# Two attentions over sixteen meta tokens: their products widened to all 128 rows of the array

## The chip, the core and the metric

The kernel runs on one core of one Trainium2 chip. The metric is device time in microseconds, from one launch. A core has a matrix engine (TensorE, "PE" in the profile, with its weight loads as "PEld"), a vector engine (VectorE, "DVE"), a scalar engine (ScalarE, "ACT"), GpSimd ("POOL") and a queue engine that issues transfers (SyncE, "SP"). They run side by side and wait for each other by semaphores. TensorE's clock has two levels, 1.2 and 2.4 GHz; the profile shows which was granted as 0.50 or 1.00.

## What is computed

Two layers over 272 tokens: 16 learned meta tokens, then 256 tokens of input. Each layer has a SwiGLU block, a token mixer and a second SwiGLU block, each with norms and a residual. The mixer runs two attentions on one projection of its input and adds them under two gates. Cut to what matters here:

```python
def fox_attention(q, k, v, log_f, key_valid):      # 8 heads of 64
    s = einsum('bhqd,bhkd->bhqk', q, k) * scale + cum_q - cum_k
    p = softmax(where(allowed, s, -inf))            # causal, blocks of 128
    return einsum('bhqk,bhkd->bhqd', p, v)

def gla_chunked(q, k, v, log_a):                    # 4 heads, keys 64, values 128, chunks of 128
    cb = cumsum(log_a)                              # per key feature
    inter = einsum('bhtk,bhkv->bhtv', q * exp(cb), state)
    att = einsum('bhtk,bhsk,bhtsk->bhts', q, k, exp(cb_t - cb_s))
    return inter + einsum('bhts,bhsv->bhtv', att, v)
```

A query of the first chunk of 128 input tokens sees the 16 meta tokens and the earlier tokens of its chunk; one of the second chunk sees the meta tokens, the whole first chunk and the earlier tokens of its own. The last layer's output of the meta tokens isn't needed.

## The kernel before

Everything is float32. The large products (projections, SwiGLU) split each weight tile into two parts (ScalarE casts at line 106, VectorE subtracts at line 112) and run three products of 128 rows by 128 columns each over 272 tokens (lines 122 to 124; 256 tokens where the meta tokens' output isn't needed). The attentions' own products take plain float32 operands; each of them stands in the trace as two passes, so that one product is two records.

The mixer (`mixer`) walks over the 33 blocks of the input projection. Before each block it issues what earlier blocks made possible: the table at lines 768 to 788 says before which block each step stands. A list scheduler then orders every engine's instructions; it may move small steps among the projection's products. SyncE loads weights ahead; GpSimd clears tiles and takes powers for the norms.

The steps that the change touches, for one layer:

- `turn_gla` (line 456): transposes the values of one of the four heads of the gated linear attention and copies them to `gv[0]` (16 meta tokens), `gv[1]`, `gv[2]` (the chunks), at line 462.
- `between_decays` (line 591) makes the decayed queries and keys between tiles (`ex`, 2 x 416 columns): the meta keys once decayed to the end of the meta tokens (for the first chunk) and once to the end of the first chunk (for the second).
- `between` (line 605) multiplies them: per head two products of 64 rows by 16 columns over 128 queries (line 612, meta keys with either chunk) and one of 64 rows by 128 columns (line 614, first chunk's keys with the second chunk's queries). Heads 0 and 2 lie in the lower 64 rows, heads 1 and 3 in the upper. Two copies bring the first kind to `am` (16 partitions, 512 columns each).
- `gla_values` (line 718): for chunk 1 and chunk 2, per head, a product with `am` (16 rows by 128 columns over 128 values), for chunk 2 one with `abc`, and one with `att` (128 by 128), all summed in PSUM (line 727).
- `weigh` (line 664), once per pair of heads of the forgetting attention: a product of the meta keys' weights `ptm` with `fvm` (32 rows by 128 columns over 256, line 667), then products with 64 columns for each head (lines 671 and 672).
- `products` and `diagonal` (lines 520 and 565), which the change leaves alone: the decayed products inside the chunks, level by level, 64 rows high (lines 535, 550, 553, 576, 578).

Around the mixer stands the norm: `Post.done` calls `inv_rms` (line 164), in which GpSimd takes a power at line 180 that the next products wait for. GpSimd clears `vm` for the mixer (line 433) just ahead of the power that ends the first SwiGLU block.

Of the kernel before, what the change touches and what calls it, by code (L numbers as in the profile page):

```python
# [27 lines left out]
# Columns of a weight tile as loaded, and as split; how many tiles of both kinds.  # L28
# [20 lines left out]
def hybrid_kernel(ctx: ExitStack, tc: tile.TileContext, xT, w_in, w_al, w_fg, w_o, w_gu1, w_dn1, w_gu2, w_dn2, w_end, g_end, vecs, consts, marks, out):  # L49
# [43 lines left out]
    # The operands of a first product, in the order of their use.  # L93
# [32 lines left out]
    def mm2(o, w, col, x, start, stop):  # L126
        """For a block whose columns 64.. repeat those before: they take the lower parts of the weights."""
        a = w[0][:, col : col + P]
        nc.scalar.copy(a[:, 64:], w[1][:, col + 64 : col + P].bitcast(F32))
        nc.tensor.matmul(o, a, x[0], start=start, stop=False)  # L130
        nc.tensor.matmul(o, a, x[1], start=False, stop=stop)

    def run(items, nk, narrow=None):
        """Products of consecutive blocks of a weight tile: (output, operand, number in its sum), nk in a sum."""
# [10 lines left out]
    def block(src, o, xh, xl, c0):  # L145
        """128 output features."""
# [3 lines left out]
    def group(srcs, outs, xh, xl, c0, narrow=None):  # L150
        """Four times 128 output features, the contraction outermost: a tile holds two rows of blocks, feature-minor."""
# [5 lines left out]
    def idle(after, k):  # L157
        """Products that nothing uses, so that the array's clock isn't throttled while it waits."""
# [5 lines left out]
    def inv_rms(parts, n, factor, warm=False):  # L164
        """factor / rms of a token, on every partition: a PSUM tile [P, n]."""
# [23 lines left out]
    def prep(l, gcol, c0, yg=None, rb=None):  # L189
        """h += yg * rb; x = h * gain in two float32r parts; 1/rms of h, per token."""  # L190
# [28 lines left out]
    class Post:  # L219
        """Takes the output blocks of a sublayer; then gives what the residual needs."""  # L220
# [28 lines left out]
    def finish(fp, hh, hl):  # L249
        """The last products and norm, tokens on the partitions."""  # L250
# [84 lines left out]

    def operands():
        """Tiles for queries and keys: rows 64.. pick a head's cumulated gate, of the query or of the key."""
# [8 lines left out]
    def mixer(l, xh, xl, rs, qa, ka, c0):  # L346
# [6 lines left out]
        with tc.tile_pool(name="mix", bufs=1) as mp, tc.tile_pool(name="tmp", bufs=2) as tp:  # L353
            wal = mp.tile([16, GH * GDK], F32, name="wal")
            nc.sync.dma_start(wal, w_al[l])

            def scratch(shape, name):
                """A tile of up to 832 columns."""
                t = tp.tile([P, 832], F32, tag="p", name=name)
# [12 lines left out]
            # -- gates of both attentions: cumulated log-sigmoids --  # L372
# [40 lines left out]
            # -- the rest of the projections --  # L413
# [15 lines left out]
            # values, tokens on the partitions; those of the meta tokens for two heads at once, block-diagonal  # L429
            fv = [mp.tile([P, 512], F32, name=f"fv{i}") for i in range(2)]  # L430
            fvm = mp.tile([2 * META, 4, P], F32, name="fvm")
# [11 lines left out]
            def turn_fox(i):  # L443
# [10 lines left out]
                nc.scalar.copy(fvm[:, i, :], t[: 2 * META, 2 * P : 3 * P])  # L454

            def turn_gla(i):
                vt = vts.pop(B_GV + i)
                t = bank("s")
                for k, (o, m) in enumerate(TILES):
                    nc.tensor.transpose(t[:m, k * P : (k + 1) * P], vt[:, o : o + m], ident)  # L460
                for k, (o, m) in enumerate(TILES):
                    nc.scalar.copy(gv[k][:, i * P : (i + 1) * P], t[:m, k * P : (k + 1) * P])
# [24 lines left out]
            # -- gated linear attention: the decayed products, level by level --  # L487
# [3 lines left out]
            def second(x, L):  # L491
                """The later half of each run of 2 L columns."""
# [26 lines left out]
            # Heads r and r + 2 hold the same rows of the array; the two r write to banks of their own.  # L519
            def products(i):  # L520
# [4 lines left out]
                if L >= 32:  # L525
                    # Few and large blocks: only those are computed.
# [59 lines left out]
            # between the tiles: meta keys with the first chunk and with the second, first chunk's keys with the second  # L586
            am = mp.tile([META, 2, 4, P], F32, name="am")
# [3 lines left out]
            def between_decays():  # L591
                nonlocal ex
                ex = scratch((2, 416), "ex")
                r1 = G[:, :, 15:16]
                r2 = G[:, :, 143:144]
                nc.vector.tensor_tensor(ex[:, :, 0:128], G[:, :, 16:144], r1.broadcast_to([P, 2, 128]), ALU.subtract)
                nc.vector.tensor_tensor(ex[:, :, 128:256], G[:, :, 144:272], r2.broadcast_to([P, 2, 128]), ALU.subtract)
                nc.vector.tensor_tensor(ex[:, :, 256:272], r1.broadcast_to([P, 2, 16]), G[:, :, 0:16], ALU.subtract)
                nc.vector.tensor_tensor(ex[:, :, 272:416], r2.broadcast_to([P, 2, 144]), G[:, :, 0:144], ALU.subtract)
                act_exp(ex, ex, scale=1.0 / 16)  # L600
                nc.vector.tensor_tensor(ex[:, :, 0:256], ex[:, :, 0:256], gq[:, :, 16:272], ALU.mult)
                nc.vector.tensor_tensor(ex[:, :, 256:272], ex[:, :, 256:272], gk[:, :, 0:16], ALU.mult)
                nc.vector.tensor_tensor(ex[:, :, 272:416], ex[:, :, 272:416], gk[:, :, 0:144], ALU.mult)

            def between():
                pm, pb = [bank("pp") for r in range(2)], [bank("s") for r in range(2)]
                for hd in range(GH):
                    r, hh = hd % 2, hd // 2
                    x = head_rows(ex, hd)
                    for k in range(2):  # L610
                        q = 2 * k + hh
# [315 lines left out]
```

## Time and profile before

| | |
|---|---|
| median of 3 runs | 1283.63 us (1282.05 to 1290.56) |
| profiled execution, first to last instruction | 1284.0 us |
| TensorE busy | 1267.3 us (99%) |
| VectorE busy | 893.2 us (70%) |
| ScalarE busy | 696.8 us (54%) |
| GpSimd busy | 31.7 us (2%) |
| mean granted TensorE clock | 0.990 |

For the profiled execution only its span is known, 1284.0 us; it stands 0.4 us above the median of the runs, and what lies around the span is taken as none. A busy TensorE is not TensorE at its peak: its products overlap, and the length of one record holds the fill and drain of the array. What a product costs is read from the distance between starts in the timeline.

### The profile page before, as it was taken

To read this page: it belongs to the slowest core of one execution; us is meant where nothing else is said; L and a number is where in the kernel's file an instruction comes from. 1 tells how busy PE (TensorE), PEld (TensorE's weight loads), DVE (VectorE), ACT (ScalarE), POOL (GpSimd) and SP (SyncE) were. 2 spreads that over 40 slices of the span, in tenths; PEclk is the share of its full clock that TensorE was granted. 3 is DMA by queue.
4 is the path that set the end of the run, shared out by engine and by line. 5 is a ranking of instruction groups with operands and counts; after the bars stand their busy time and mean duration, and the time that the engine had idled before them with its cause. 6 is when DMAs were issued, how large, how long until landed. Compare 5 with 4: busy or idle time off the path is not lost.

```text
span 1284.0 us, 25316 instructions
## 1 busy us (share of the span) xinstructions
PE 1267.3 (99%) x9866; PEld 1225.9 (95%) x9866; DVE 893.2 (70%) x1831; ACT 696.8 (54%) x1447; POOL 31.7 (2%) x35
## 2 busy tenths in 40 slices
PE   7999999999999999999999999999999999999997
PEld 7999999888899999999999999999898999999986
DVE  7777656886456777776568777558985687877652
ACT  7555444764355556554446555446754554755551
POOL 2000000000000100000000000001000000000000
PEclk9999999998899999999999999999999999999999
DMA  9655553532235545555535555563433465565550
GB/s 313 205 173 175 164 176 126 173 113 82 67 117 174 180 133 175 179 170 160 181 132 187 178 178 163 170 193 133 137 100 115 133 189 172 181 187 191 181 164 33
DMA packets 58199, 203.88 MB, mean 159 GB/s; under 512 B 6688, under 2 KB 8000, under 8 KB 58048
## 3 DMA queue, kind: packets, MB, share of 16 engines
q1 hardware_dynamic: 57376, 201.19, 49.6%
q8 instruction: 78, 1.28, 0.4%
q10 hardware_dynamic: 576, 0.80, 0.3%
q0 software_dynamic: 128, 0.28, 0.1%
q14 instruction: 41, 0.34, 0.1%
HBM read 200.92 MB, written 1.05 MB: 157 GB/s over the span
## 4 chain that ended last, share of the span: by engine, by line
PE 82%; issue 14%; DMA 1%; ACT 1%; SPq 0%; DVE 0%; POOL 0%; ACTq 0%; DVEq 0%; POOLq 0%
PE mm L122 13%; PE mm L124 12%; PE mm L123 12%; PE pp L122 7%; PE pp L124 7%; PE pp L123 7%; PE s L122 5%; PE s L123 5%; PE s L124 5%; PE pp L550 1%; PE po L727 1%; PE s L161 1%; PE s L633 1%; DMA w<-in_w_gu 1%; PE po L183 1%
## 5 line engine op out<-in xcount | busy, mean ns | idle before, releaser
L106 ACT CAST wh<-w 128x512 fp32r<-128x512 f32 (+1 forms) x768 | 464.6, 613 | 423.9 <-PE mm L123 194.6
L112 DVE TENSOR_TENSOR wl<-w,wh 128x512 fp32r<-128x512 f32 (+1 forms) x768 | 516.1, 681 | 254.2 <-ACT wh L106 238.6
L122 PE MATMUL mm<-xh,wh 128*128 128x272 f32 (+1 forms) x1072 | 313.1, 295 | 7.2 <-ACT wh L106 6.4
L124 PE MATMUL mm<-xh,wl 128*128 128x272 f32 (+1 forms) x1072 | 311.8, 292 | 0.2 <-DVE wl L112 0.2
L123 PE MATMUL mm<-xl,wh 128*128 128x272 f32 (+1 forms) x1072 | 311.0, 291 | 0.0
L122 PEld LDWEIGHTS mm<-xh,wh 128*128 128x128 f32 x1072 | 205.2, 193 | 9.1 <-ACT wh L106 6.4
L123 PEld LDWEIGHTS mm<-xl,wh 128*128 128x128 f32 x1072 | 206.2, 192 | 1.2 <-issue 0.9
L124 PEld LDWEIGHTS mm<-xh,wl 128*128 128x128 f32 x1072 | 205.6, 192 | 1.8 <-issue 1.1
L124 PE MATMUL s<-xh,wl 128*128 128x272 f32 (+1 forms) x496 | 142.2, 287 | 0.0
L123 PE MATMUL s<-xl,wh 128*128 128x272 f32 (+1 forms) x496 | 142.0, 287 | 0.0
L122 PE MATMUL s<-xh,wh 128*128 128x272 f32 (+1 forms) x496 | 141.0, 288 | 0.0
L124 PE MATMUL pp<-xh,wl 128*128 128x272 f32 (+1 forms) x480 | 137.1, 289 | 0.0
L123 PE MATMUL pp<-xl,wh 128*128 128x272 f32 (+1 forms) x480 | 137.0, 288 | 0.0
L122 PE MATMUL pp<-xh,wh 128*128 128x272 f32 (+1 forms) x480 | 134.0, 288 | 0.0
L123 PEld LDWEIGHTS s<-xl,wh 128*128 128x128 f32 x496 | 93.4, 188 | 0.1
L124 PEld LDWEIGHTS s<-xh,wl 128*128 128x128 f32 x496 | 93.4, 188 | 0.0
L122 PEld LDWEIGHTS s<-xh,wh 128*128 128x128 f32 x496 | 92.8, 188 | 0.1
L123 PEld LDWEIGHTS pp<-xl,wh 128*128 128x128 f32 x480 | 90.9, 189 | 0.0
L124 PEld LDWEIGHTS pp<-xh,wl 128*128 128x128 f32 x480 | 90.7, 190 | 0.0
L122 PEld LDWEIGHTS pp<-xh,wh 128*128 128x128 f32 x480 | 89.3, 190 | 0.0
L122 PE MATMUL pp<-hh,wh 128*128 128x272 f32 x264 | 76.1, 288 | 0.0
L122 PE MATMUL mm<-hh,wh 128*128 128x272 f32 x264 | 76.1, 288 | 0.0
(287 smaller groups left out, 2140.4 us busy)
## 6 DMA issues: line engine op xcount, KB each, us to landing
w<-in_w_gu SPq DMA_DIRECT2D x175, 512.0 KB, 3.6
w<-in_w_in SPq DMA_DIRECT2D x82, 512.0 KB, 3.5
w<-in_w_dn SPq DMA_DIRECT2D x48, 512.0 KB, 3.5
w<-in_w_end SPq DMA_DIRECT2D x22, 512.0 KB, 3.7
w<-in_w_dn SPq DMA_DIRECT2D x24, 384.0 KB, 3.2
w<-in_w_fg SPq DMA_DIRECT2D x16, 512.0 KB, 3.5
w<-in_w_o SPq DMA_DIRECT2D x16, 512.0 KB, 3.4
h<-in_xT SPq DMA_DIRECT2D x8, 136.0 KB, 4.8
```

Source lines behind the costliest of these rows:

```text
L106: i = nc.scalar.copy(wh[:, :n], w[:, a:b])
L112: nc.vector.tensor_tensor(wl[:, :n], w[:, a:b], wh[:, :n].bitcast(F32), ALU.subtract)
L122: nc.tensor.matmul(o, a, x[0], start=start, stop=False)
L123: nc.tensor.matmul(o, a, x[1], start=False, stop=False)
L124: nc.tensor.matmul(o, b, x[0], start=False, stop=stop)
L161: m = nc.tensor.matmul(o[:, :P], ident, ident, start=True, stop=True)
L183: last = nc.tensor.matmul(bc[:, o : o + m], rp[:m, j : j + 1].broadcast_to([m, P]), ident[:m, :m], start=True, stop=True)
L550: nc.tensor.matmul(pp[r][:, q * 64 : q * 64 + 64].rearrange("p (b l) -> p b l", l=L), x[:, o : o + P], second(x[:, o : o + P], L), start=T ...
L633: nc.tensor.matmul(s[:, c : c + e], qa[:104, hd, q0:e], ka[:104, hd, 0:e], start=True, stop=True)
L727: nc.tensor.matmul(o[:, hd, :], a, gv[kv][:, hd * P : (hd + 1) * P], start=i == 0, stop=i == len(terms) - 1)
```

## The change

- `am` is now one tile of 128 partitions by 256 columns (the queries of both chunks). Each head owns 32 of the partitions: 16 for its meta keys, the other 16 hold whatever the product gave for the next 16 keys.
- A tile `gvm` (128 by 512) is cleared by GpSimd, and `turn_gla` copies each head's meta values to that head's partitions and columns. So one product `am` x `gvm`, 128 rows by 128 columns over 512, does the meta keys of all four heads of a chunk, and opens the sum in PSUM; the other products follow. In the last layer the copy to `gv[0]` isn't made; in the first layer the copy to `gvm` is added to it.
- In `between` the meta keys are decayed to the end of the meta tokens alone, and one product per head (64 rows by 32 columns, each head with array columns of its own, over 256 queries) replaces two. The queries of both chunks are decayed from the end of the meta tokens; the second chunk's queries stand in `ex` once more, decayed from the end of the first chunk. `ex` has 2 x 528 columns instead of 2 x 416. The four products with meta keys stand ahead of the four others in the code.
- `fvm` and the two `ptm` tiles get 128 partitions, cleared by GpSimd at the start of the mixer; only the first 32 are ever written. The product of line 667 so has 128 rows.
- Comments are taken out.

```diff
+    def slot(hd):
+        return 64 * (hd % 2) + 32 * (hd // 2)
...
+            gvm = mp.tile([P, 512], F32, name="gvm")
+            fvm = mp.tile([P, 4, P], F32, name="fvm")
+            ptms = [mp.tile([P, SEQ], F32, name=f"ptm{i}") for i in range(2)]
+            for t in (gvm, fvm, *ptms):
+                nc.gpsimd.memset(t, 0.0)
...
-            fvm = mp.tile([2 * META, 4, P], F32, name="fvm")
...
-                nc.scalar.copy(fvm[:, i, :], t[: 2 * META, 2 * P : 3 * P])
+                nc.scalar.copy(fvm[: 2 * META, i, :], t[: 2 * META, 2 * P : 3 * P])
...
+                nc.scalar.copy(gvm[slot(i) : slot(i) + META, i * P : (i + 1) * P], t[:META, :P])
                 for k, (o, m) in enumerate(TILES):
-                    nc.scalar.copy(gv[k][:, i * P : (i + 1) * P], t[:m, k * P : (k + 1) * P])
+                    if k or not c0:
+                        nc.scalar.copy(gv[k][:, i * P : (i + 1) * P], t[:m, k * P : (k + 1) * P])
...
-            am = mp.tile([META, 2, 4, P], F32, name="am")
+            am = mp.tile([P, 2 * P], F32, name="am")
...
-                ex = scratch((2, 416), "ex")
+                ex = scratch((2, 528), "ex")
...
-                nc.vector.tensor_tensor(ex[:, :, 0:128], G[:, :, 16:144], r1.broadcast_to([P, 2, 128]), ALU.subtract)
-                nc.vector.tensor_tensor(ex[:, :, 128:256], G[:, :, 144:272], r2.broadcast_to([P, 2, 128]), ALU.subtract)
-                nc.vector.tensor_tensor(ex[:, :, 256:272], r1.broadcast_to([P, 2, 16]), G[:, :, 0:16], ALU.subtract)
-                nc.vector.tensor_tensor(ex[:, :, 272:416], r2.broadcast_to([P, 2, 144]), G[:, :, 0:144], ALU.subtract)
+                nc.vector.tensor_tensor(ex[:, :, 0:256], G[:, :, 16:272], r1.broadcast_to([P, 2, 256]), ALU.subtract)
+                nc.vector.tensor_tensor(ex[:, :, 256:384], G[:, :, 144:272], r2.broadcast_to([P, 2, 128]), ALU.subtract)
+                nc.vector.tensor_tensor(ex[:, :, 384:400], r1.broadcast_to([P, 2, 16]), G[:, :, 0:16], ALU.subtract)
+                nc.vector.tensor_tensor(ex[:, :, 400:528], r2.broadcast_to([P, 2, 128]), G[:, :, 16:144], ALU.subtract)
                 act_exp(ex, ex, scale=1.0 / 16)
...
-                    for k in range(2):
-                        q = 2 * k + hh
-                        nc.tensor.matmul(pm[r][:META, q * P : (q + 1) * P], x[:, 256 + 16 * k : 272 + 16 * k],
-                                         x[:, k * P : (k + 1) * P], start=True, stop=True)
-                    nc.tensor.matmul(pb[r][:, hh * P : (hh + 1) * P], x[:, 288:416], x[:, P : 2 * P], start=True, stop=True)
+                    nc.tensor.matmul(pm[r][slot(hd) : slot(hd) + 32, : 2 * P], x[:, 384:416], x[:, : 2 * P], start=True, stop=True)
+                for hd in range(GH):
+                    r, hh = hd % 2, hd // 2
+                    x = head_rows(ex, hd)
+                    nc.tensor.matmul(pb[r][:, hh * P : (hh + 1) * P], x[:, 400:528], x[:, 2 * P : 3 * P], start=True, stop=True)
                 for r in range(2):
-                    nc.scalar.copy(am[:, r], pm[r][:META].rearrange("p (q t) -> p q t", q=4))
+                    nc.scalar.copy(am[64 * r : 64 * r + 64], pm[r][64 * r : 64 * r + 64, : 2 * P])
...
-                ptm = tp.tile([2 * META, SEQ], F32, tag="ptm", name="ptm")
+                ptm = ptms[b % 2]
...
-                o = bank("po")[:m].rearrange("p (h v) -> p h v", h=GH)
+                o = bank("po")
+                if k:
+                    nc.tensor.matmul(o, am[:, (k - 1) * P : k * P], gvm, start=True, stop=False, skip_group_check=True)
+                o = o[:m].rearrange("p (h v) -> p h v", h=GH)
...
-                             1: [(am[:, r, hh, :], 0), (att[:, r, hh, :], 1)],
-                             2: [(am[:, r, 2 + hh, :], 0), (abc[:, r, hh, :], 1), (att[:, r, 2 + hh, :], 2)]}[k]
+                             1: [(att[:, r, hh, :], 1)],
+                             2: [(abc[:, r, hh, :], 1), (att[:, r, 2 + hh, :], 2)]}[k]
```

The list scheduler orders the rest anew. Three places on TensorE show what that does; a row is the line, the output and operand tiles and the output's shape, "x4" is four in a row. In these rows lines 612 and 614 of before are lines 622 and 626 of the change, 550 is 562, 460 is 470, 655 is 667.

The products between the tiles (`between`) of the first layer, before:

```order
L124 MATMUL mm<-xh,wl 128x272
L612 MATMUL pp<-ex 16x128 x2
L614 MATMUL s<-ex 128x128
L612 MATMUL pp<-ex 16x128 x2
L614 MATMUL s<-ex 128x128
L612 MATMUL pp<-ex 16x128 x2
L614 MATMUL s<-ex 128x128
L612 MATMUL pp<-ex 16x128 x2
L614 MATMUL s<-ex 128x128
L122 MATMUL mm<-xh,wh 128x272
```

and in the change:

```order
L123 MATMUL mm<-xl,wh 128x272
L124 MATMUL mm<-xh,wl 128x272
L622 MATMUL pp<-ex 32x256 x4
L626 MATMUL s<-ex 128x128 x4
L122 MATMUL mm<-xh,wh 128x272
L123 MATMUL mm<-xl,wh 128x272
```

The narrow and the wide products alternated four times; now all narrow ones stand first.

The same place of the second layer, before:

```order
L124 MATMUL mm<-xh,wl 128x256
L614 MATMUL s<-ex 128x128
L612 MATMUL pp<-ex 16x128 x2
L614 MATMUL s<-ex 128x128
L612 MATMUL pp<-ex 16x128 x4
L614 MATMUL s<-ex 128x128
L612 MATMUL pp<-ex 16x128 x2
L614 MATMUL s<-ex 128x128
L122 MATMUL mm<-xh,wh 128x256
```

and in the change:

```order
L124 MATMUL mm<-xh,wl 128x256
L626 MATMUL s<-ex 128x128
L622 MATMUL pp<-ex 32x256 x2
L626 MATMUL s<-ex 128x128
L622 MATMUL pp<-ex 32x256 x2
L626 MATMUL s<-ex 128x128 x2
L122 MATMUL mm<-xh,wh 128x256
```

Here the scheduler still mixes them: two narrow groups instead of three, each between wide products.

The last level's products of the second layer (`L550`) and the transposes of the fourth pair of heads and of the values near it, before:

```order
L656 MATMUL s<-con,pk 32x128 x2
L460 MATMUL s<-con,vt 128x128
L124 MATMUL mm<-xh,wl 128x272
L550 MATMUL pp<-E 128x64 x8
L460 MATMUL s<-con,vt 16x128
L460 MATMUL s<-con,vt 128x128 x2
L122 MATMUL mm<-xh,wh 128x256
```

and in the change:

```order
L124 MATMUL mm<-xh,wl 128x272
L562 MATMUL pp<-E 128x64 x4
L667 MATMUL s<-con,p 128x128
L562 MATMUL pp<-E 128x64
L667 MATMUL s<-con,p 128x128 x5
L668 MATMUL s<-con,pk 32x128 x2
L470 MATMUL s<-con,vt 16x128
L470 MATMUL s<-con,vt 128x128 x2
L562 MATMUL pp<-E 128x64 x3
L470 MATMUL s<-con,vt 16x128
L470 MATMUL s<-con,vt 128x128 x2
L122 MATMUL mm<-xh,wh 128x256
```

The eight products stood in one piece; now the fox transposes cut them into three.

## Rows read from the trace of the kernel before

**Rows 1.** Page, busy time: us, share of the span, instructions.

```profile
PE 1267.3 (99%) x9866; PEld 1225.9 (95%) x9866; DVE 893.2 (70%) x1831; ACT 696.8 (54%) x1447; POOL 31.7 (2%) x35
```

**Rows 2.** Waits of PE between 240 and 430 us: us in total, times, longest.

```profile
PE s L633 <- DMA ka<-sm: 1.3, 1, 1.3
```

**Rows 3.** Stretches: engines' busy us (count), granted PE clock, DMA share, GB/s.

```profile
288.82:295.65 6.83, 6.83 (x46) 5.77 (x45) 3.79 (x13) 2.22 (x6) 0.00 (x0) 0.50 0.22 74
...
333.19:336.61 3.42, 3.42 (x17) 3.28 (x17) 1.38 (x4) 0.00 (x0) 0.00 (x0) 0.50 0.45 153
991.97:995.38 3.41, 3.41 (x17) 3.41 (x18) 0.17 (x1) 1.63 (x9) 1.01 (x1) 0.50 0.33 133
995.38:998.79 3.41, 3.41 (x31) 3.41 (x31) 2.43 (x5) 1.77 (x4) 0.00 (x0) 1.00 0.00 0
```

**Rows 4.** Timeline of PE, `gla_values`, second layer: start us, us, line, tiles, rows*columns, moving.

```profile
988.91 0.48 PE L727 MATMUL po<-gv,am 16*128 16x128 f32 x2
989.32 0.49 PE L727 MATMUL po<-gv,att 128*128 128x128 f32 x2
989.74 0.48 PE L727 MATMUL po<-gv,am 16*128 16x128 f32 x2
...
999.89 0.48 PE L727 MATMUL po<-gv,am 16*128 16x128 f32 x2
...
1000.95 0.48 PE L727 MATMUL po<-gv,am 16*128 16x128 f32 x2
```

**Rows 5.** Timeline of PE, first `weigh` of the first layer.

```profile
269.44 0.29 PE L122 MATMUL mm<-xh,wh 128*128 128x272 f32 x1
269.66 0.69 PE L667 MATMUL po<-ptm,fvm 32*128 32x256 f32 x2
270.28 0.66 PE L671 MATMUL po<-pt,fv 128*64 128x256 f32 x4
270.76 0.40 PE L672 MATMUL po<-pt,fv 128*64 128x128 f32 x4
```

**Rows 6.** `between`: the stretch it fills in either layer; timeline, second layer.

```profile
344.59:348.49 3.90, 3.90 (x26) 2.35 (x24) 1.55 (x3) 2.19 (x5) 0.00 (x0) 1.00 0.30 86
979.69:983.07 3.38, 3.38 (x26) 2.10 (x24) 1.53 (x4) 2.18 (x5) 0.00 (x0) 1.00 0.27 62
...
980.20 0.61 PE L612 MATMUL pp<-ex 64*16 64x128 f32 x4
980.74 0.48 PE L614 MATMUL s<-ex 64*128 64x128 f32 x2
981.15 0.62 PE L612 MATMUL pp<-ex 64*16 64x128 f32 x8
981.71 0.48 PE L614 MATMUL s<-ex 64*128 64x128 f32 x2
```

**Rows 7.** Timeline of PE, `diagonal`, second layer.

```profile
975.59 1.26 PE L576 MATMUL pp<-gq,gk 64*128 64x128 f32 x16
976.78 0.39 PE L122 MATMUL mm<-xh,wh 128*128 128x256 f32 x1
```

**Rows 8.** Timeline of POOL: start us, us, line, tile; idle before and what ended it.

```profile
0.91 0.95 POOL L333 MEMSET att<- 128x1024 f32 x1
...
211.08 0.13 POOL L433 MEMSET vm<- 128x32 f32 x1 [190.77 <-PE mm L124]
212.64 0.85 POOL L180 TENSOR_TENSOR rp<-ms,nhalf 128x3 f32<-128x3 f32 x1 [1.44 <-DVE ms L179]
...
869.53 0.85 POOL L180 TENSOR_TENSOR rp<-ms,nhalf 128x3 f32<-128x3 f32 x1 [1.50 <-DVE ms L179]
```

**Rows 9.** ACT groups by line and shape: busy us, mean ns, idle before.

```profile
L462 ACT COPY gv<-s 16x128 f32<-16x128 f32 x8 | 2.0, 252 | 2.4 <-PE s L460 2.4
L351 ACT ACTIVATE ex<-ex 128x832 f32<-128x832 f32 x2 | 1.8, 898 | 0.0
```

More of the change, by code (lines that the diff above doesn't have):

```diff
@@ L355, in mixer @@
             nc.sync.dma_start(wal, w_al[l])
+            gvm = mp.tile([P, 512], F32, name="gvm")
[3 more added lines that the diff above has]
+                nc.gpsimd.memset(t, 0.0)
             def scratch(shape, name):
-                t = tp.tile([P, 832], F32, tag="p", name=name)
+                t = tp.tile([P, 1056], F32, tag="p", name=name)
                 k = int(np.prod(shape))
@@ L592, in between_decays @@
                 nonlocal ex
-                ex = scratch((2, 416), "ex")
+                ex = scratch((2, 528), "ex")
                 r1 = G[:, :, 15:16]
                 r2 = G[:, :, 143:144]
-                nc.vector.tensor_tensor(ex[:, :, 0:128], G[:, :, 16:144], r1.broadcast_to([P, 2, 128]), ALU.subtract)
-                nc.vector.tensor_tensor(ex[:, :, 128:256], G[:, :, 144:272], r2.broadcast_to([P, 2, 128]), ALU.subtract)
-                nc.vector.tensor_tensor(ex[:, :, 256:272], r1.broadcast_to([P, 2, 16]), G[:, :, 0:16], ALU.subtract)
-                nc.vector.tensor_tensor(ex[:, :, 272:416], r2.broadcast_to([P, 2, 144]), G[:, :, 0:144], ALU.subtract)
+                nc.vector.tensor_tensor(ex[:, :, 0:256], G[:, :, 16:272], r1.broadcast_to([P, 2, 256]), ALU.subtract)
+                nc.vector.tensor_tensor(ex[:, :, 256:384], G[:, :, 144:272], r2.broadcast_to([P, 2, 128]), ALU.subtract)
+                nc.vector.tensor_tensor(ex[:, :, 384:400], r1.broadcast_to([P, 2, 16]), G[:, :, 0:16], ALU.subtract)
+                nc.vector.tensor_tensor(ex[:, :, 400:528], r2.broadcast_to([P, 2, 128]), G[:, :, 16:144], ALU.subtract)
                 act_exp(ex, ex, scale=1.0 / 16)
                 nc.vector.tensor_tensor(ex[:, :, 0:256], ex[:, :, 0:256], gq[:, :, 16:272], ALU.mult)
-                nc.vector.tensor_tensor(ex[:, :, 256:272], ex[:, :, 256:272], gk[:, :, 0:16], ALU.mult)
-                nc.vector.tensor_tensor(ex[:, :, 272:416], ex[:, :, 272:416], gk[:, :, 0:144], ALU.mult)
+                nc.vector.tensor_tensor(ex[:, :, 256:384], ex[:, :, 256:384], gq[:, :, 144:272], ALU.mult)
+                nc.vector.tensor_tensor(ex[:, :, 384:528], ex[:, :, 384:528], gk[:, :, 0:144], ALU.mult)
             def between():
@@ L660, in turn_scores @@
                         nc.vector.tensor_copy(pt[:, r, :], t[:, :384])
-                    nc.scalar.copy(ptm[:, r * P : (r + 1) * P], t[: 2 * META, 384:512])
+                    nc.scalar.copy(ptm[: 2 * META, r * P : (r + 1) * P], t[: 2 * META, 384:512])
                 turned[b] = pt, ptm
@@ L705, in meta_weigh @@
                 for b in range(4):
-                    nc.tensor.matmul(o[:, b * META : (b + 1) * META], fvm[:, b, :], pmT[:, b * META : (b + 1) * META], start=True, stop=True)
+                    nc.tensor.matmul(o[:, b * META : (b + 1) * META], fvm[: 2 * META, b, :], pmT[:, b * META : (b + 1) * META], start=True, stop=True)
                 o = o[:, : 4 * META].rearrange("p (b q) -> p b q", b=4)
@@ L723, in gla_values @@
                     terms = {0: [(att0[:, r, hh, :], 0)],
-                             1: [(am[:, r, hh, :], 0), (att[:, r, hh, :], 1)],
-                             2: [(am[:, r, 2 + hh, :], 0), (abc[:, r, hh, :], 1), (att[:, r, 2 + hh, :], 2)]}[k]
+                             1: [(att[:, r, hh, :], 1)],
+                             2: [(abc[:, r, hh, :], 1), (att[:, r, 2 + hh, :], 2)]}[k]
                     for i, (a, kv) in enumerate(terms):
-                        nc.tensor.matmul(o[:, hd, :], a, gv[kv][:, hd * P : (hd + 1) * P], start=i == 0, stop=i == len(terms) - 1)
+                        nc.tensor.matmul(o[:, hd, :], a, gv[kv][:, hd * P : (hd + 1) * P], start=not k, stop=i == len(terms) - 1, skip_group_check=True)
                 ss = tp.tile([P, 4], F32, tag="ss", name="ss")
```

## The prediction

> **What bounds the kernel now.** I read the page's busy times first: TensorE is busy 99% of the span, VectorE 70%, ScalarE 54%, GpSimd 2% [rows 1]. Then TensorE's waits: its longest wait in the first mixer is 1.3 us, for a transfer that the change doesn't touch [rows 2]. So TensorE's queue is the path, and what counts is how long each product holds it. Third, the stretches by granted clock: in five of them it stands at 0.50, which is 1.2 GHz. Four lie in the first layer's mixer (6.83, 3.41, 6.83 and 3.42 us, 20.5 in all, first and last shown), one in the second layer's, 991.97 to 995.38 [rows 3]. That one holds 17 products where the next stretch of the same length, at 1.00, holds 31: a stretch costs half its length, 1.7 us per 3.4 us piece. There are seven such pieces, 11.9 us. What TensorE did right before 991.97 is `gla_values` of chunk 1 [rows 4]; before of the first layer's four stand level products, 64 rows high, which stay as they are. Last I read the timeline of TensorE where the change works [rows 4 to 7], and POOL's where it clears tiles [rows 8].
>
> **What a small product costs.** In `gla_values` one head of chunk 1 takes 989.74 - 988.91 = 0.83 us with four passes; one of chunk 2 takes 1000.95 - 999.89 = 1.06 us with six [rows 4]. Both alternate once between 16 rows and 128 rows. Two more passes cost 0.23, so a pass over 128 columns costs some 0.11; what is left of 0.83 for the two changes of shape is 0.19 each. The same appears at `weigh`: projection products follow each other every 0.11 to 0.12 us (31 in 3.41) [rows 3], yet the one of 32 rows starts 0.22 after the last of them (269.44 to 269.66), and its two passes over 256 columns (0.44 by the price above) take 0.62 [rows 5]: some 0.1 in which the array empties, and some 0.1 for a weight load that nothing covers. The Trainium skill states the first half of this in "TensorEngine Tiling (Array Packing)", Key Properties: changing the tiling mode drains the engine. By that rule, with no price on the page, only the number of changes counts; the trace agrees, with 0.19 us each.
>
> **The change, part by part.**
>
> 1. `gla_values`. Before, eight changes of shape per call (am, att for each of four heads). After, one product of 128 rows over 512 columns and then products of 128 rows: no change of shape at all. The columns stay the same: four times two passes over 128 become two over 512; no row of before shows a float32 pass over 512 columns, but cost by column holds from 128 to 256 (0.11 and 0.21 to 0.22), and I take 0.44. Saved: 8 x 0.19 = 1.5 us per call; two chunks, two layers: 6.1 us. Bounds: 0 if height is free (rival 3), 6.6 at 0.20 to 0.21.
>
> 2. `between`. In the timeline a narrow group of four passes lasts 0.54 until the next wide pair, a wide pair 0.41 until the next narrow group, and eight narrow passes of two heads 0.56 (981.15 to 981.71) [rows 6]: heads in different row halves run side by side. `weigh` shows the same for different columns: four passes over 256 with 64 columns each last 0.48 (270.28 to 270.76) instead of 0.88 [rows 5]. So four narrow heads, each with array columns of its own, should last as long as one: two passes over 256, 0.44, plus 0.10. The wide ones of different row halves pair up: 16 passes of `diagonal` take 1.19 us [rows 7], so 0.12 a pair after 0.2 for entry and exit. First layer: 0.09 + 0.54 + (4 x 0.12 + 0.2) = 1.3 against 3.90: 2.6 saved. Second layer, in the scheduler's order (wide, two narrow, wide, two narrow, two wide): 0.09 + 0.41 + 0.54 + 0.41 + 0.54 + 0.43 = 2.4 against 3.38: 1.0 saved. Together 3.6; without running side by side 1.4 (rival 2).
>
> 3. `weigh`. The product of line 667 gets 128 rows, so the change of shape ahead of it goes where it follows a full-height product: six of eight; the fourth pair of either layer stands behind a product of another shape in both kernels. The change into 64 columns behind it stays. 6 x 0.19 = 1.1 us.
>
> 4. New order. Counted over the orders of both kernels, the stretch around the fourth pair of the second layer has two changes of shape more (the eight level products cut into three pieces against one), that of the first layer one more: 3 x 0.19 = 0.6 us lost.
>
> 5. GpSimd clears 1536 columns more per mixer. 1024 columns took 0.95 us, so 1.4 us. They come where `vm` is cleared, at 211.08, released by the same product, ahead of the power that TensorE's next products wait for. That power waits for VectorE anyway: idle 1.44 us before it, 1.50 in the second layer [rows 8]. I take 0; the slack is just used up. Should the clearing run at half that speed, it would cost 1.4 us a layer, 2.8 in all, since nothing else covers the power.
>
> 6. ScalarE and VectorE. Four copies of 0.25 us more in the first layer, `ex` wider by 224 columns (0.9 us for 832 now, so 0.24) [rows 9], VectorE's steps on `ex` wider in proportion; the copies to `am` get shorter. TensorE hardly waits for either engine, and both have room [rows 1, 2]. I take 0. If their cover went, it would be 1.3 us of ScalarE in the first layer.
>
> Sum without the clock: 6.1 + 3.6 + 1.1 - 0.6 = 10.2 us. The span of the profiled execution is 1284.0, 0.4 above the median of the runs; so 1273.8.
>
> **The clock.** The piece at 991.97 follows 3.3 us in which 16-row and 128-row products alternated and half the time was emptying and loading [rows 4]. After, that place is 1.8 us of full-height products. I count this piece as gone: 1.7 us. The other six pieces belong to work that stays. But where such pieces fall differs between executions: three runs of one program lie 8.5 us apart, five pieces' worth. The groups of `between` and of the other `gla_values` look like the one that was caught and ran at full clock here [rows 4, 6]; another execution may catch them and spare level products. So seven is a draw from both kinds of place, and only one kind is left after the change. I take five pieces, two fewer: 3.4 us. Forecast: 1273.8 - 3.4 = 1270.4.
>
> **Rivals.**
>
> 1. The clock gives nothing back: as many pieces, at other places. For it: six of seven are at level products. Against: the seventh isn't. 1273.8 us.
>
> 2. The narrow heads don't run side by side, because two of them share their row half. Then the first layer's eight passes over 256 columns take 1.76 instead of 0.44, the second layer's two groups 0.88 instead of 0.44 each: 2.2 us more, 1272.6. Against it: the two heads of `weigh` share all their rows and overlap [rows 5].
>
> 3. Height is free, so filling it changes nothing: a product of 16 or 32 rows would cost what one of 128 does, whatever stands around it. Then parts 1 and 3 bring nothing and only `between` is left: 1270.4 + 7.2 = 1277.6. Against it: head times of 0.83 and 1.06 that passes alone can't fill [rows 4]. The Trainium skill has this rule in "TensorE: Matmul & The Clock Gate", section LDWEIGHTS (loading the stationary operand): a load of 32 rows takes as long as one of 128, since only columns count. The trace bears it out for a pass by itself, but not for a neighbour of another shape.
>
> 4. Slower: the new order is worse for the clock. Around the fourth pair both layers now have long runs of transposes, level products and small products without a projection product between them; the second layer, which had no piece there, could get them as the first layer has. Each piece costs 1.7 us; six more than now eat up the 10.2 us, and with seven more (14 in all) the time is 1273.8 + 7 x 1.7 = 1285.7. For it: the first layer lost its pieces at just such runs. Against: the second layer has no meta queries and so few tiny products.
>
> **How the numbers follow.** Forecast 0.55, with one to five pieces fewer: 1265.3 to 1272.1. Rival 1: 0.24. Rival 2: 0.09. Rival 3: 0.07. Rival 4: 0.05. The range starts with five pieces fewer and a saving of `gla_values` at its upper bound (1264.8) and ends at rival 3 (1277.6), which takes in rivals 1 and 2 and part 5 at half speed: 1264 to 1278. About 1% can be told from no change, here 12.8 us: faster means below 1270.8. The forecast lies at that edge, with more of its cases below than above: 0.53 faster, 0.43 within 1%, 0.04 slower.
>
> **What would show it.** In the changed kernel's timeline: `gla_values` of the second layer, chunk 1, from its first small product to the next projection product in about 1.8 us instead of 3.3; `between` in 1.3 and 2.4 us; the first product of `weigh` some 0.12 us after the projection product before it; the power of line 180 still waiting for VectorE, not for clearing; no piece at 0.50 right behind `gla_values`. I am wrong if the 512-column product takes more than 0.5 us a pass, if four narrow heads take more than 0.8 us, or if the pieces at 0.50 number seven or more.

## The result and the profile after

| | before | changed |
|---|---|---|
| median | 1285.79 us (1282.05 to 1290.56, 4 runs) | 1268.89 us (1267.79 to 1269.59, 4 runs) |
| profiled execution | 1284.0 us span, mean granted clock 0.990 | 1268.24 us, span 1266.4, clock 0.997 |

The ratio is 0.9874, with a 95% interval from 0.985 to 0.9899: faster by 1.0 to 1.5%. The forecast of 1270.4 us lies 1.5 us above the measured median.

First the page's busy times of the changed kernel, beside [rows 1]:

```profile
PE 1247.4 (99%) x9826; PEld 1210.2 (96%) x9826; DVE 893.4 (71%) x1831; ACT 697.5 (55%) x1451; POOL 34.9 (3%) x43
```

TensorE has lost 19.9 us of busy time and 40 records, and it is still the path: beside its weight loads (PEld) no busy time changed by more than 4 us. PE's longest waits, grouped by who ended them (us in total, times, longest), first before and then changed, show that no new wait in the mixers took the place of the old work:

```profile
PE mm L122 <- ACT wh L106: 6.4, 1, 6.4
PE s L633 <- DMA ka<-sm: 2.1, 2, 1.3
...
PE mm L122 <- ACT wh L106: 8.7, 2, 6.2
PE s L645 <- DMA ka<-sm: 2.1, 2, 1.1
```

The first kind is at the program's start, where TensorE waits for its first weights in every kernel here; in this execution a second such wait of 2.5 us comes to it. The second is the transfer of [rows 2], under its new line number; the change doesn't touch it. Next a stretch of 3.4 us near the start, then the two mixers (busy us and count of PE, PEld, DVE, ACT, POOL, then granted PE clock, DMA share, GB/s):

```profile
16.62:20.03 3.41, 3.38 (x13) 3.15 (x14) 3.40 (x8) 3.00 (x7) 0.00 (x0) 0.50 1.03 414
240.00:400.00 160.00, 158.62 (x1274) 146.42 (x1273) 113.37 (x270) 92.68 (x239) 3.01 (x3) 1.00 0.39 120
...
897.00:1010.00 113.00, 113.00 (x962) 104.69 (x963) 85.22 (x206) 69.36 (x186) 2.01 (x2) 1.00 0.42 129
```

The same two mixers of before, over the same times, stand at a mean clock of 0.94 and 0.98, with 1177 and 907 records of products in place of 1274 and 962. All seven half-clock pieces of the mixers [rows 3] are gone from this one execution; the only piece before 1000 us is the one at 16.62, right behind the second wait for weights. Eight of the twelve profiles of this study have a piece that starts between 16 and 17 us.

Now PE's timeline at the four places that the prediction named, in order of time (start us, duration of the group, line, tiles, rows*columns of the held operand, moving operand, count): the first `weigh`, one level's products of the first layer, `between` of the first and of the second layer, `gla_values` of chunk 1 of the second.

```profile
271.52 0.29 PE L122 MATMUL mm<-xh,wh 128*128 128x272 f32 x1
271.65 0.59 PE L679 MATMUL po<-ptm,fvm 128*128 128x256 f32 x2
272.17 0.66 PE L683 MATMUL po<-pt,fv 128*64 128x256 f32 x4
...
287.70 0.66 PE L562 MATMUL pp<-E 64*128 64x64 f32 x4
288.29 0.20 PE L565 MATMUL pp<-E 64*16 64x8 f32 x2
288.42 0.66 PE L562 MATMUL pp<-E 64*128 64x64 f32 x4
...
337.51 0.29 PE L124 MATMUL mm<-xh,wl 128*128 128x272 f32 x1
337.73 0.64 PE L622 MATMUL pp<-ex 64*32 64x256 f32 x8
338.30 0.71 PE L626 MATMUL s<-ex 64*128 64x128 f32 x8
338.94 0.39 PE L122 MATMUL mm<-xh,wh 128*128 128x272 f32 x1
...
967.23 0.28 PE L124 MATMUL mm<-xh,wl 128*128 128x256 f32 x1
967.44 0.49 PE L626 MATMUL s<-ex 64*128 64x128 f32 x2
967.86 0.62 PE L622 MATMUL pp<-ex 64*32 64x256 f32 x4
...
969.80 0.39 PE L122 MATMUL mm<-xh,wh 128*128 128x256 f32 x1
...
975.47 0.28 PE L124 MATMUL mm<-xh,wl 128*128 128x256 f32 x1
975.59 1.02 PE L734 MATMUL po<-gvm,am 128*128 128x512 f32 x2
976.44 1.05 PE L742 MATMUL po<-gv,att 128*128 128x128 f32 x8
977.25 0.36 PE L122 MATMUL mm<-xh,wh 128*128 128x256 f32 x1
```

A group's own duration overlaps the next group, so what counts is the distance from one start to the next. `gla_values` takes 977.25 - 975.59 = 1.66 us, where before the same call began at 988.91 [rows 4] and lasted until 992.16, 3.25 us:

```profile
991.82 0.69 PE L727 MATMUL po<-gv,att 128*128 128x128 f32 x2
992.16 0.56 PE L122 MATMUL mm<-xh,wh 128*128 128x256 f32 x1
```

The two passes over 512 columns take 0.85. `between` of the first layer takes 338.94 - 337.73 = 1.21, and 0.1 more ahead of its first product, where [rows 6] has 3.90. In the second layer it is 969.80 - 967.44 = 2.36 and 0.1, against 3.38. The product of line 679 starts 0.13 us behind the projection product, where its 32-row forerunner started 0.22 behind it [rows 5], and its two passes last 0.52 instead of 0.62. Last, POOL's timeline at the start of the first mixer and of the second (start us, us, line, tile; idle before and what ended it):

```profile
213.33 0.53 POOL L366 MEMSET gvm<- 128x512 f32 x1 [190.55 <-PE mm L124]
213.80 0.53 POOL L366 MEMSET fvm<- 128x512 f32 x1
214.26 0.57 POOL L366 MEMSET ptm<- 128x256 f32 x2
214.76 0.13 POOL L443 MEMSET vm<- 128x32 f32 x1
214.89 0.85 POOL L180 TENSOR_TENSOR rp<-ms,nhalf 128x3 f32<-128x3 f32 x1
...
855.50 0.53 POOL L366 MEMSET gvm<- 128x512 f32 x1 [185.11 <-PE mm L124]
...
857.13 0.85 POOL L180 TENSOR_TENSOR rp<-ms,nhalf 128x3 f32<-128x3 f32 x1
```

The power comes 214.89 - 213.33 = 1.56 us behind the product that releases POOL; before it was 212.64 - 211.08 = 1.56 [rows 8]. The clearing fits into the wait for VectorE to within what the rows resolve.

### The profile page after: what moved, and what is told of

It is laid out like the page before. It is cut to its first block, busy times and chain, and to the rows that moved or that the text cites. A ratio compares the mean times of both kernels' runs of the same rounds, so it can differ in the third digit from the quotient of the medians.

```text
span 1266.4 us, 25250 instructions
## 1 busy us (share of the span) xinstructions
PE 1247.4 (99%) x9826; PEld 1210.2 (96%) x9826; DVE 893.4 (71%) x1831; ACT 697.5 (55%) x1451; POOL 34.9 (3%) x43
## 4 chain that ended last, share of the span: by engine, by line
PE 82%; issue 14%; DMA 1%; ACT 1%; POOL 0%; SPq 0%; ACTq 0%; DVE 0%; DVEq 0%; POOLq 0%
PE mm L122 13%; PE mm L124 12%; PE mm L123 12%; PE pp L122 7%; PE pp L124 7%; PE pp L123 7%; PE s L122 5%; PE s L123 5%; PE s L124 5%; PE pp L562 1%; PE s L161 1%; PE s L645 1%; DMA w<-in_w_gu 1%; PE po L183 1%; DMA ka<-sm 1%
## 5 line engine op out<-in xcount | busy, mean ns | idle before, releaser
L122 PE MATMUL mm<-xh,wh 128*128 128x272 f32 (+1 forms) x1072 | 309.4, 291 | 9.6 <-ACT wh L106 8.7
L123 PE MATMUL mm<-xl,wh 128*128 128x272 f32 (+1 forms) x1072 | 307.8, 288 | 0.0
L122 PEld LDWEIGHTS mm<-xh,wh 128*128 128x128 f32 x1072 | 201.7, 189 | 11.7 <-ACT wh L106 8.9
L123 PEld LDWEIGHTS mm<-xl,wh 128*128 128x128 f32 x1072 | 202.9, 189 | 1.2 <-issue 0.9
L124 PEld LDWEIGHTS mm<-xh,wl 128*128 128x128 f32 x1072 | 202.2, 189 | 1.6 <-issue 1.1
```

The lines of the kernel that those rows point to most:

```text
L123: nc.tensor.matmul(o, a, x[1], start=False, stop=False)
L124: nc.tensor.matmul(o, b, x[0], start=False, stop=stop)
```

## The experiments

The profiled pair differs by 17.6 us of span, more than the forecast's 13.2. Two executions of one kernel differ by some 10 us at most, so the question was how much of the gain is work saved and how much is where the half-clock pieces happened to fall. Each run lists its span and its mean granted clock, and the records hold two levels, 1.00 and 0.50. So 2 x (1 - mean clock) x span is a run's time at 0.50, its **half-clock time**: 1 - 0.997 over 1266.4 us makes 7.6 us. (The clock is listed to three digits, so it comes in steps of 2.5 us.) Over all 112 runs of the study that list their clock, of nine different kernels, a straight line with a base of its own for each row of the table below and one slope for all gives

time = base + 0.41 us for each us of half-clock time,

and leaves 0.56 us of scatter per run. The base is the time that the line gives for no time at half clock. The bases compare kernels at equal clock, which the medians don't. I take them as good to about 0.5 us.

| kernel | median us (runs) | ratio to before [95%] | mean half-clock time, us | base, us | half-clock stretches of its profile in the mixers: start us, first; second |
|---|---|---|---|---|---|
| before | 1285.79 (4) | | 22.3 (12.8 to 33.5, 46 runs beside the others) | 1275.6 | 288.8, 305.9, 319.5, 333.2; 992.0 |
| the same again | 1283.25 (12) | 0.9993 [0.9975, 1.0011] | 20.1 | 1275.7 | 317.3, 331.0; 989.8 |
| changed | 1268.89 (4) | 0.9874 [0.985, 0.9899] | 8.9 | 1265.1 | none; none |
| changed, again | 1272.27 (4) | 0.9902 [0.9888, 0.9917] | 16.5 | 1265.0 | 289.9, 307.0; none |
| changed, a third time | 1268.33 (6) | 0.9874 [0.9854, 0.9895] | 8.9 | 1264.7 | 290.2, 303.8; none |
| weigh_low | 1274.82 (4) | 0.9923 [0.9893, 0.9952] | 21.0 | 1266.3 | 289.7, 306.7, 320.4, 337.5; none |
| weigh_alone | 1281.09 (9) | 0.9974 [0.9959, 0.9988] | 16.8 | 1274.6 | 289.1, 306.1, 343.7; 988.8 |
| gla_alone | 1275.50 (7) | 0.9935 [0.9914, 0.9957] | 16.8 | 1269.5 | 316.4, 336.9; none |
| gla_four | 1269.20 (4) | 0.9881 [0.9866, 0.9896] | 8.9 | 1265.4 | 333.9; none |
| between_alone | 1280.47 (7) | 0.9971 [0.9957, 0.9985] | 18.6 | 1272.7 | 290.0, 320.7; 986.3 |
| between_mixed | 1276.44 (4) | 0.9928 [0.9904, 0.9952] | 15.9 | 1269.1 | 291.4, 305.1, 342.6; none |
| levels_grouped | 1260.24 (5) | 0.9815 [0.9791, 0.984] | 4.5 | 1258.7 | none; none |

A stretch in the last column is one to three pieces of 3.41 us long.

**The kernel before, unedited.** How far do pieces and times move by themselves?

> The kernel before, unedited, to see where its half-clock pieces fall from run to run. Draw theory (pieces fall by chance): mean granted clock differs between runs, from about 0.985 to 0.995, times spread over 8 us, and the profile shows the pieces at other places than 288.8, 305.9, 319.5, 333.2 and 992.0 us. Place theory (the pieces belong to those products): every run has 0.989 to 0.991 and the profile shows the same five stretches.

No difference, as it must be. But the clock differs from run to run (0.988 to 0.996), and the pieces of its profile stand in part elsewhere. From its stretches (columns as above):

```profile
317.30:324.10 6.80, 6.80 (x33) 6.29 (x33) 1.77 (x7) 1.97 (x8) 0.00 (x0) 0.50 0.00 0
...
989.80:993.20 3.40, 3.40 (x17) 3.40 (x17) 0.17 (x1) 1.73 (x9) 1.01 (x1) 0.50 0.30 120
```

Nothing at 288.8 or 305.9, where the other execution of the same program had pieces; two stretches at 317.3 and 331.0 that overlap those at 319.5 and 333.2; one again at `gla_values` of the second layer. In the first mixer a profile's pieces are one draw.

**The changed kernel, twice more.**

> The changed kernel, unedited, for its clock over more runs. In the runs so far its half-clock time was 7.6 to 10.1 us (start and end of the kernel alone), that of before 10 to 31 us. Theory that full height keeps both mixers at full clock: every run again between 7 and 11 us, 1267 to 1270 us. Draw theory: some runs with 14 us or more, up to 1275 us.

> The changed kernel once more beside it, for its clock. Draw theory: half-clock time between 7 and 18 us, 1268 to 1273 us, other than in one of the two earlier groups of runs. Place theory: one value in all runs.

The bases agree to 0.4 us; the medians differ by 3.9 us, since the half-clock time does (8.9, 16.5, 8.9). The first profile's empty first mixer was luck: both repeats have two stretches there, at level products.

**The product of `weigh` back to 32 rows** (weigh_low), the order of the instructions being the same:

```diff
-                nc.tensor.matmul(o[:, :SEQ], fvm[:, b, :], ptm, start=True, stop=False)
+                nc.tensor.matmul(o[:, :SEQ], fvm[: 2 * META, b, :], ptm[: 2 * META], start=True, stop=False)
```

> The changed kernel with the product of the meta keys in weigh back at 32 rows; nothing else differs, and the order of all instructions is the same. Shape theory: six more changes of shape at 0.19 us, so 1.1 us more than the changed kernel (1268.9): 1270.0, clock 0.996 to 0.997. Theory that the height of this product keeps the first mixer at full clock: at least two pieces at half clock come back there, clock 0.994 or less, 1273 us or more. Theory that height is free: 1268.9.

PE's timeline at the first `weigh`:

```profile
270.55 0.29 PE L122 MATMUL mm<-xh,wh 128*128 128x272 f32 x1
270.77 0.69 PE L679 MATMUL po<-ptm,fvm 32*128 32x256 f32 x2
271.40 0.66 PE L683 MATMUL po<-pt,fv 128*64 128x256 f32 x4
```

The start is late by 0.22 again and the passes take 0.63, as in [rows 5]: 0.20 us more than in the changed kernel, at the price of one change of shape. Its base is 1.2 to 1.6 us above the three of the changed kernel (1266.3 against 1264.7 to 1265.1): six to eight such places. Its median, though, is 5.9 us above the changed kernel's: the rest is the clock, with up to 33.2 us at 0.50 in a run. So the base came out as the shape theory had it, while the median and the half-clock time came out as the second theory had them. Whether 32-row products bring more pieces or four runs drew badly stays open: the four runs had 33.2, 17.8, 25.5 and 7.6, and the changed kernel's fourteen had 5.1 to 17.8.

**Full-height `weigh` alone, put into before** (weigh_alone):

```diff
+            fvm = mp.tile([P, 4, P], F32, name="fvm")
+            ptms = [mp.tile([P, SEQ], F32, name=f"ptm{i}") for i in range(2)]
+            for t in (fvm, *ptms):
+                nc.gpsimd.memset(t, 0.0)
...
-                ptm = tp.tile([2 * META, SEQ], F32, tag="ptm", name="ptm")
+                ptm = ptms[b % 2]
```

> The kernel before with the full-height product of weigh alone. Over runs of equal half-clock time: shape theory 1.1 us less than before. Clock: if the height of this product is what keeps the first mixer's clock, half-clock time falls from 22 us in the mean to 13 or less; if each of the three places only adds its share, to 16 to 20 us: about 1282 us.

The base falls by 1.0 us. From both sides the part is worth 1.0 to 1.6. The half-clock time, 16.8 us, is in the range of the second theory, that each place adds its share; the 15 runs of before beside it have 22.1 in the mean.

**The wide product of `gla_values` alone** (gla_alone). The small products of `between` stay, and their results are copied to each head's partitions:

```diff
+                    for hh in range(2):
+                        z = 64 * r + 32 * hh
+                        nc.scalar.copy(am[z : z + META], pm[r][:META].rearrange("p (k h t) -> p h k t", k=2, h=2)[:, hh])
...
+                if k:
+                    nc.tensor.matmul(o, am[:, k - 1], gvm, start=True, stop=False, skip_group_check=True)
...
-                             1: [(am[:, r, hh, :], 0), (att[:, r, hh, :], 1)],
+                             1: [(att[:, r, hh, :], 1)],
```

> The kernel before with the wide full-height product of gla_values alone (am still made by the old products, copied to the heads' partitions). Shape theory: 32 changes of shape fewer, 6.1 us, and the piece behind gla_values of the second layer gone: 1.7 us; the first mixer keeps its pieces: about 1278 us against 1285.8. Theory that height is free: no difference beyond the clock's spread. Theory that the meta products set the whole clock: the first mixer's pieces go as well, 1268 to 1270 us.

The base falls by 1275.6 - 1269.5 = 6.1 us, so this one part is more than half of what the change saves. And the second mixer of its profile has no piece at 0.50. The last column of the table shows the same for all twelve profiles: all four profiles with the old `gla_values` have a piece there, and none of the eight with the new one has any piece in the second mixer. So this piece is bound to the place. It begins at 992.0, 989.8, 988.8 and 986.3 us, and in PE's timelines of these four kernels the last two passes of chunk 1's call begin within 0.6 us of it, at 991.82, 989.57, 988.22 and 986.35. The first mixer keeps its pieces (316.4 and 336.9).

**Four full-height products in place of the wide one** (gla_four). Does the width matter, or only that no shape changes?

```diff
-                    nc.tensor.matmul(o, am[:, (k - 1) * P : k * P], gvm, start=True, stop=False, skip_group_check=True)
+                    for hd in range(GH):
+                        z = slice(hd * P, (hd + 1) * P)
+                        nc.tensor.matmul(o[:, z], am[:, (k - 1) * P : k * P], gvm[:, z], start=hd == 0, stop=False, skip_group_check=True)
```

> The changed kernel with the one wide product of gla_values split into four full-height products of 128 columns, one per head. Shape theory: the passes cover the same columns and no shape changes, so within 0.3 us of the changed kernel, 1268.9. Theory that the number of products sets the price (three products, six passes fewer per call at about 0.11 us): 2.6 us more.

PE's timeline at the same call:

```profile
976.59 1.05 PE L736 MATMUL po<-gvm,am 128*128 128x128 f32 x8
977.48 1.06 PE L744 MATMUL po<-gv,att 128*128 128x128 f32 x8
978.29 0.36 PE L122 MATMUL mm<-xh,wh 128*128 128x256 f32 x1
```

1.70 us from the first small product to the next projection product, against 1.66 with one wide product; the base is 0.4 us above that of the changed kernel run beside it. Eight passes of 128 columns cost what two of 512 do. So the gain doesn't come from the smaller number of products. What both forms share is that no shape changes within the call; whether low products standing together, without being filled up, would have done as well was not tried.

**The new `between` alone** (between_alone), its results copied into the old layout of `am` for the old `gla_values`:

```diff
+                    nc.tensor.matmul(pm[r][slot(hd) : slot(hd) + 32, : 2 * P], x[:, 384:416], x[:, : 2 * P], start=True, stop=True)
+                for hd in range(GH):
...
+                    nc.tensor.matmul(pb[r][:, hh * P : (hh + 1) * P], x[:, 400:528], x[:, 2 * P : 3 * P], start=True, stop=True)
```

> The kernel before with the new products of between alone (am then copied to the layout of before, gla_values as before). Grouping theory: 3.5 us less than before at equal half-clock time (the opposite edit cost 3.9 us), half-clock time 17 to 22 us, about 1281 us. If between is short only next to the other edits: under 2 us.

The base falls by 2.9 us, nearer to the grouping theory's 3.5 than to the other's "under 2".

**The narrow products of `between` among the wide ones again** (between_mixed): two of 128 queries per head, each head's followed by its wide one.

```diff
-                    nc.tensor.matmul(pm[r][slot(hd) : slot(hd) + 32, : 2 * P], x[:, 384:416], x[:, : 2 * P], start=True, stop=True)
-                for hd in range(GH):
-                    r, hh = hd % 2, hd // 2
-                    x = head_rows(ex, hd)
+                    for k in range(2):
+                        nc.tensor.matmul(pm[r][slot(hd) : slot(hd) + 32, k * P : (k + 1) * P], x[:, 384:416], x[:, k * P : (k + 1) * P], start=True, stop=True)
```

> The changed kernel with the narrow products of between split in two again (two of 128 columns per head, 32 array columns each) and issued head by head with the wide ones, as before. If grouping and running side by side is what made this place short: 3.5 us more than the changed kernel (1272.4), the place at 3.9 and 3.4 us. If the place is short because there are fewer columns or products, half of that or less: under 1270.7. Clock as the changed kernel, 0.996.

PE's timeline in the first layer:

```profile
339.44 0.62 PE L623 MATMUL pp<-ex 64*32 64x128 f32 x4
339.99 0.48 PE L624 MATMUL s<-ex 64*128 64x128 f32 x2
340.40 0.62 PE L623 MATMUL pp<-ex 64*32 64x128 f32 x4
340.95 0.48 PE L624 MATMUL s<-ex 64*128 64x128 f32 x2
341.37 0.62 PE L623 MATMUL pp<-ex 64*32 64x128 f32 x4
...
343.80 0.59 PE L122 MATMUL mm<-xh,wh 128*128 128x272 f32 x1
```

Each head takes 340.40 - 339.44 = 0.96 us; the four took 4.36, the last of them partly inside the piece at 342.6. The changed kernel does the same arithmetic in 1.21. The base is 4.1 us above that of the changed kernel run twice elsewhere (1269.1 against 1265.0). So it isn't the 32 columns that cost, but narrow products that stand between wide ones: there the shape changes at every step and the heads don't run side by side (0.96 us each, one after another). This run doesn't part the two.

**A step further: the meta tokens' tiny products behind the large ones** (levels_grouped). In `products` and in `diagonal` of the first layer every head's two large products are followed by a product of the meta tokens with an output of 16 by 8 or 16 by 16. Here these come in a loop of their own behind all four heads:

```diff
                         nc.tensor.matmul(pp[r][:, q * 64 : q * 64 + 64].rearrange("p (b l) -> p b l", l=L), x[:, o : o + P],
                                          second(x[:, o : o + P], L), start=True, stop=True)
+                for hd in range(GH):
+                    r, hh = hd % 2, hd // 2
+                    x = head_rows(E, hd)
                     if meta:
```

> The changed kernel with the meta tokens' tiny products of the levels and the diagonal (16 by 8 and 16 by 16 outputs, first layer) issued behind the four heads' large ones instead of between them. Shape theory: some 24 changes of shape fewer and row halves that pair up, about 5 us less than the changed kernel at equal half-clock time. Clock: if the half-clock pieces of the first mixer come from the stretches in which these products alternate, they go: 7 to 11 us in every run, near 1264 us. If changes of shape cost only next to 16-row weights: no gain.

PE's timeline of the level that stands at 287.70 in the changed kernel:

```profile
285.98 1.10 PE L562 MATMUL pp<-E 64*128 64x64 f32 x14
287.01 0.33 PE L673 MATMUL s<-con,p 128*128 128x128 f32 x1
287.27 0.43 PE L562 MATMUL pp<-E 64*128 64x64 f32 x2
...
288.62 0.21 PE L568 MATMUL pp<-E 64*16 64x8 f32 x4
...
289.71 0.39 PE L122 MATMUL mm<-xh,wh 128*128 128x272 f32 x1
```

Fourteen passes of level products now take 1.03 us, where the changed kernel spent 0.72 on four and the two tiny passes behind them (288.42 - 287.70). The stretch to the next projection product takes 3.7 us; in the changed kernel it goes from 287.70 to 292.65, 5.0 us. The base falls by another 6.0 us against the changed kernel run beside it (1258.7 against 1264.7), where the shape theory said 5. The half-clock time falls to 4.5 us on average, 2.5 to 7.6 in its five runs, and no piece stands in either mixer of its profile; the only one is at the program's end. That bears out the clock theory, by which the first mixer's pieces come from the stretches where these products alternate. It is the fastest kernel here, 1.6 to 2.1% faster than before.

## Why the prediction was right

The work saved is 1275.6 - 1265.0 = 10.6 us at equal clock, where the sum said 10.2. The parts by themselves, 6.1, 2.9 and 1.0, add up to 10.0; so they hardly depend on each other, to within what the bases resolve.

1. `gla_values`, 6.1 predicted, 6.1 measured. The pass over 512 columns, which no row of before showed, takes 0.43 us (0.44 taken). The price of 0.19 per change of shape holds.
2. `between`, 3.6 predicted; 3.5 by the timeline ((3.90 - 1.31) + (3.38 - 2.46)), 2.9 alone and 4.1 undone by the bases. The four narrow heads take 338.30 - 337.73 = 0.57 us, where 0.54 was taken: they run side by side.
3. `weigh`, 1.1 predicted, 1.0 to 1.6 measured.
4. The new order, 0.6 lost: not tried by itself. The parts put in one by one add up to 0.6 less than the whole, which leaves no loss; undone one by one (`between` 4.1, `weigh` 1.2 to 1.6) they leave up to 1.2. It stays open.
5. GpSimd's clearing, nothing: right in price, but with no slack left. The sign that the power would still wait for VectorE doesn't show: it starts at 214.89 with POOL never idle, when the clearing ends (214.76 + 0.13) and VectorE's step for it has just ended (214.60 + 0.21).
6. ScalarE and VectorE, nothing: PE's waits show no new one.

**The clock** is the term that was mis-sized: "I take five pieces, two fewer: 3.4 us". Over 58 runs of before (the 46 beside the others and the 12 of the same again) and 14 of the changed kernel the mean half-clock time fell from 21.8 to 11.1 us. That is 10.7 / 3.41 = 3.1 pieces fewer, and by the slope a piece costs 0.41 x 3.41 = 1.4 us, not 1.7. Together 4.4 us instead of 3.4. The step that counted too few is the one that left the first layer's pieces where they were. The second layer's piece is gone from all eight profiles with the new `gla_values`, as forecast; that is one of the 3.1. The rest must have gone elsewhere, and weigh_alone shows some of it: its profile still has the second layer's piece, and yet its half-clock time is 5.3 us below that of before beside it. How the rest divides between the places stays open. That a half-clock us costs less than 0.5 fits with time in which TensorE's columns aren't what lasts (waits at the start, the array emptying), but this was only argued.

**Luck in the number.** The forecast started from 1284.0 us, the span of one execution, as if nothing lay around it; every run listed here is 1.8 to 2.4 us longer than its span. And that execution had 25.7 us at half clock, more than the mean of before. From a time of some 1286 us, 10.6 of work and (25.7 - 11.1) x 0.41 = 6.0 of clock give 1269.4, near the 1268.9 measured. The forecast began 2 us too low and took off 2.6 us too little for the clock; the two errors nearly cancel.

Rival 1, no clock back, is refuted by the half-clock times, which fell by half. Rival 2 is refuted by the 0.57 us. Rival 3, height is free, is refuted twice: by gla_alone (6.1 where it says 0, and gla_four shows that the smaller number of products isn't what gained it) and by weigh_low (0.20 us at one place with nothing else changed). The rule of the Trainium skill that stood beside it ("TensorE: Matmul & The Clock Gate", section LDWEIGHTS) speaks of one load; what these runs price is the neighbour of another shape. Rival 4, more pieces by the new order, is refuted by the same half-clock times, and all three profiles of the changed kernel run the second mixer, where it feared new pieces, at full clock.

The profiled pair's 17.6 us of span follow too: before lists 0.990, the changed kernel 0.997, so 25.7 us at half clock against 7.6. That is 18.1 x 0.41 = 7.4 us, and with 10.6 saved 18.0.

## What to carry to other kernels

Where TensorE is the path, list its products by shape in the order of the queue and count the places where the shape changes: each cost about 0.19 us here, more than a pass over 128 columns. Two remedies worked, filling low products with zeros to full height and grouping those of one shape. At the one place where the number of products was changed by itself (gla_four) it mattered little. Judge a change of under 1% at equal clock: take the half-clock time of many runs, since one profile shows one draw of the pieces.

## What was not expected of the hardware

- Products that use different rows or columns of the array run side by side even when they were issued one after another. [rows 5 and 6] had shown it for two heads; here it held for four: eight narrow passes over 256 columns of four heads took 0.57 us (337.73 to 338.30), where eight in a row at 0.21 would take 1.7.
- The granted clock fell to 0.50, 1.2 GHz, while TensorE was busy all the time: the stretch 317.30 to 324.10 of the kernel before is busy for 6.80 of 6.80 us. Mostly small and low products ran from 312.75 on and through its first 3 us; the rest of it was full-height projection products, by then at half clock. One program's runs had between 10.2 and 33.5 us at that level.

```profile
316.90 1.51 PE L706 MATMUL s<-pmT,fvm 32*128 32x16 f32 x8
...
320.30 0.57 PE L122 MATMUL mm<-xh,wh 128*128 128x272 f32 x1
```

- The smallest products were among the dearest: the meta tokens' products with outputs of 16 by 8 and 16 by 16, moved behind their neighbours without a change of their arithmetic, gave 6.0 us at equal clock, as much as the whole of `gla_values`.
